# Gathering 80 instead of 72 expert rows early, eight instead of six per round, in a hybrid attention and retrieval layer

## The chip, the cores and the metric

The kernel runs on one core of a Trainium2 chip, in one launch. The metric is device time in microseconds, and lower is better. Engines are named as the profile names them: PE is TensorE (PEld its weight loads), DVE is VectorE, ACT is ScalarE, POOL is GpSimd and SP is SyncE.

## What is computed

One decoder layer on 512 tokens of width 1024, in float32:

```python
proj = x @ w_in                       # 1024 x 3072: q, k, v of two groups of 8 heads
oa = dilated_window_attention(qa, ka, va)   # windows (128,1), (512,4), (2048,16)
ob = stick_breaking_attention(qb, kb, vb)
x = layer_norm(ALPHA * x + concat(oa, ob) @ w_out)
# PEER: 8 heads, two top-16 of 128 keys each, then 16 of 256 sums
scores = einsum('bshpc,hpnc->bshpn', (x @ w_query), sub_keys)
expert_idx, gates = ...               # 8 x 16 = 128 of 16384 experts per token
h = einsum('td,ted->te', x, expert_u[expert_idx])
act = gates * gelu(h)
y = einsum('te,ted->td', act, expert_v[expert_idx])
x = layer_norm(ALPHA * x + y)
```

## The kernel before

The tokens are four blocks of 128. The experts are reached in two ways. For blocks 2 and 3 the whole tables `uT` and `peer_v` are streamed in 128 chunks of 128 experts each, and PE multiplies all of them (`h_mm` L969, `y_mm` L1318, with the gates spread out to a dense map). For blocks 0 and 1 only the chosen experts are fetched: each of a token block's 128 choices is one indirect gather of 128 rows (one row of 1024 floats per token, 512 KB in all), issued on POOL (L834), and DVE uses it in one instruction over 128x1024 elements: a dot product with x for `peer_u` (L852), a scaled addition for `peer_v` (L864). "A row" below is one such gather with its use. There are 512 of them, numbered in the order in which they are used: 0 to 127 are `peer_u` for block 0, 128 to 255 `peer_v` for block 0, and 256 to 511 the same for block 1. `issue()` keeps several gathers ahead of the use, as many as there are buffers less one: 7 buffers (pools `gat` and `g3`) for the early rows and 9 (`gat` and `g2`) later.

The rows are spread by hand over the other work of the kernel:

1. Input projection and attention of block 0, then its first routing. At its end the choices of block 0 are known and gathering can begin.
2. **The early stage**, which the change touches. The projection of blocks 1 to 3 (`project_in`, generator `proj`) loads the weights in pieces of 128x1024. For exactness in the fast PE format each piece is split in a high half on ACT (`wh`, L129) and a low half on DVE (`wl`, L133), and each product is three matmuls (L136, L137, L138, where L138 or L137 reads `wl`). Beside it the dilated heads of blocks 1 to 3 run (`heads_a`: PE L353, DVE L356, ACT L359, PE L363, ACT L366, PE L369), and the early rows are gathered and used. `mix` takes steps from the three in turn: `MIXB` gives how many of each, and `PRE0` how many rows are done in the stage. 18 rows are done before the mixing, the rest in it. `first_new` starts the first two stick-breaking heads.
3. The stick-breaking heads (PE L377 to L397, ACT L383 to L393, DVE L387), output projection (L575) and normalization, with 2 or 3 rows per step (`take`).
4. The query projection and the routing of blocks 1 to 3, with rows between the steps; chunks of `uT` are multiplied ahead.
5. **The final loop** over the chunks: per chunk `h_mm` of chunk c+36, `y_mm` of chunk c, the loads of a `uT` and a `peer_v` chunk, and as many rows as a proportion asks for (`goal`), so that all 512 are done by chunk 118. After chunk 91 there are no `uT` chunks left and only `y_mm` runs.

Between stages 2 and 5 the number of rows taken is fixed by the code: 160 of them. With 72 rows early, 232 are done when the final loop begins and 280 are left for it.

When row 127 has been used, the 128 dot products of block 0 go through Gelu in `close_dots` (ACT L842, with a table load before it and one after it, L844), and DVE multiplies them by the gates (L859) before it uses row 128. `close_dots` is called by the use of row 128, or in the code right after stage 3's heads, whichever is first.

Inside the early stage's mixing the order of each engine's instructions is set by the tile framework's own scheduler from the program's order; stages 3 to 5 are in the order written.

Of the kernel before, what the change touches and what calls it, by code (L numbers as in the profile page):

```python
# [79 lines left out]
TG = 4  # L80
LEAD = 36
KT = 6
MIXB = (6, 4, 4)
PRE0 = 72
QGATH = 3
QH = 2
PRE1 = 7
# [14 lines left out]
def build(ctx, nc, tc, a):  # L102
# [316 lines left out]
    def heads_a(tb, done):  # L419
        return heads(tb, done, head_a, close_a, 0)  # L420
# [72 lines left out]
    def until(main, side, ratio):  # L493
        n = 0
        for _ in main:
            n += 1
            while n >= ratio:
                n -= ratio
                next(side, None)

    def chain(*steps):
        for s_ in steps:
            yield from s_

    def run(*steps):
        ratio = steps[-1] if isinstance(steps[-1], tuple) else (1,) * len(steps)
        for _ in mix(*steps[:len(ratio)], ratio):
            pass

    def mix(*steps):  # L510
        ratio = steps[-1]
        live = [(s_, r) for s_, r in zip(steps, ratio)]
        while live:
            for s_, r in list(live):
                for _ in range(r):
                    if next(s_, s_) is s_:
                        live.remove((s_, r))
                        break
                    yield

    def head(steps, n):
        for _ in range(n):
            if next(steps, steps) is steps:
                return
            yield
# [299 lines left out]
    def gather(n):  # L825
        tb, kind, j = n // (2 * P), n // P % 2, n % P
        if n < PRE0:
            pool, nm, more = g3, "g3", GB3
# [42 lines left out]
    def issue():  # L871
        nonlocal issued
        ahead_ = GB1 + (GB2 if g2 else GB3 if issued < PRE0 else 0)
        while issued < min(done + ahead_ - 1, limit):
            gus[issued] = gather(issued)
            issued += 1

    def gathers(n):
        nonlocal done
        if n == PRE0:  # L880
            issue()
            yield
        while done < n:
            issue()
            gather_use(done, gus.pop(done))
            done += 1
            yield
# [165 lines left out]
    rest = []  # L1053
    limit = PRE0 + GB1 - 1
    early = gathers(PRE0)
    until(mix(route_steps(0, 4, 4), head(early, PRE1), (2, 1)), proj, 1)
# [15 lines left out]
    def first_new():  # L1072
        for j, n in ((0, 3), (1, 2)):
            begin(j)
            for _ in range(n):
                go(j)
            yield

    run(early, proj, chain(*(heads_a(tb, rest) for tb in PARTS[1]), first_new()), MIXB)
    qws.close()  # L1080
# [381 lines left out]
```

## Time and profile before

| | us |
|---|---|
| median of 3 runs | 1426.12 (1420.84 to 1427.63) |
| the profiled execution's own time | 1424.04 |
| its span | 1422.3 |
| PE busy in the span | 1366.6 (96%) |
| DVE busy | 1164.9 (82%) |
| POOL busy | 656.1 (46%) |
| moved by DMA | 497.16 MB, mean 350 GB/s |

The span is the profiled execution from its first to its last instruction; its own time includes 1.7 us around it. Busy shares are means over stages that have different limits, so the stages are read apart. Where the text quotes stretches of time, they count from the start of the span. In tables of stretches, the number after "x" counts the instructions in the stretch, "PEclk" is the granted TensorE clock as a share of full speed, and "DMA share" the mean busy share of the 16 DMA engines, which reaches 1.03 where they are full. In a timeline a bracket at a row's end tells how long the engine sat idle before the instruction and what ended that.

### The profile page before, as it was taken

How to read it: one execution, taken by the hardware profiler on the slowest of the kernel's cores; microseconds unless marked ns; L12 is line 12 of the kernel's file. 1: busy time of each engine (PE TensorE's matmuls, PEld its weight loads, DVE VectorE, ACT ScalarE, POOL GpSimd, SP SyncE). 2: the span in 40 equal slices, each digit the busy share in tenths (PEclk: the TensorE clock that was granted, in tenths of full speed). 3: DMA queues.
4: the chain of work that ended last, by engine and by line, in shares of the span. 5: the costliest groups of instructions: out<-in, count | busy, mean ns of one | idle time of the engine just before them, and what ended most of it. 6: DMA issues, size and time to landing. Idle time of an engine off the chain costs nothing.

```text
span 1422.3 us, 19497 instructions
## 1 busy us (share of the span) xinstructions
PE 1366.6 (96%) x6664; PEld 1100.6 (77%) x6664; DVE 1164.9 (82%) x2381; ACT 484.0 (34%) x1008; POOL 656.1 (46%) x526
## 2 busy tenths in 40 slices
PE   8999999999999999999999999999999999998897
PEld 4677877676679998888888888888778888886555
DVE  0269998869899999899988778778788878878888
ACT  1323344364411111899522222222222222214122
POOL 0003676668553332113465555555555555652520
PEclk9999999999999999999999999999999999999999
DMA  8798998799989998779999999999999999999792
GB/s 294 246 316 277 329 367 304 272 395 359 331 315 362 334 319 281 248 238 323 344 410 409 410 410 409 409 410 410 410 410 410 409 410 410 409 410 406 289 393 87
DMA packets 163874, 497.16 MB, mean 350 GB/s; under 512 B 16544, under 2 KB 48688, under 8 KB 163648
## 3 DMA queue, kind: packets, MB, share of 16 engines
q0 software_dynamic: 74304, 270.13, 50.1%
q1 hardware_dynamic: 87744, 220.16, 41.7%
q10 hardware_dynamic: 1728, 5.64, 1.0%
q8 instruction: 52, 0.85, 0.2%
q14 instruction: 46, 0.38, 0.1%
HBM read 478.83 MB, written 16.84 MB: 349 GB/s over the span
## 4 chain that ended last, share of the span: by engine, by line
DMA 36%; PE 35%; DVE 14%; issue 11%; POOL 2%; ACT 2%; SPq 0%; DVEq 0%; POOLq 0%; ACTq 0%
DMA g<-peer_u,eidx 17%; DMA g<-peer_v,eidx 16%; PE y L1318 6%; PE h L969 3%; PE a L685 3%; PE b L685 3%; PE m L280 2%; POOL g L834 2%; PE m L138 2%; PE m L137 2%; PE m L136 1%; DVE x L864 1%; DVE g L852 1%; DMA w<-peer_v 1%; DVE yg L864 1%
## 5 line engine op out<-in xcount | busy, mean ns | idle before, releaser
L834 POOL DMA_INDIRECT g<-peer_v,eidx x256 | 313.4, 1224 | 379.1 <-DVE yg L864 100.6
L834 POOL DMA_INDIRECT g<-peer_u,eidx x256 | 336.8, 1316 | 327.2 <-DVE topi L624 121.7
L969 PE MATMUL h<-xf,w 128*128 128x256 f32 x2048 | 470.5, 379 | 0.9 <-ACT gl L961 0.9
L969 PEld LDWEIGHTS h<-xf,w 128*128 128x128 f32 x2048 | 382.1, 190 | 52.6 <-ACT gl L961 1.3
L852 DVE SCALAR_TENSOR_TENSOR g<-g,x 128x1024 f32<-128x1024 f32 x256 | 307.5, 1221 | 75.0 <-DMA g<-peer_u,eidx 74.3
L1318 PE MATMUL y<-vh,a 128*128 128x512 f32 x864 | 270.2, 416 | 18.6 <-ACT a L1301 18.3
L1318 PEld LDWEIGHTS y<-vh,a 128*128 128x128 f32 x864 | 161.9, 190 | 62.8 <-ACT a L1301 25.0
L864 DVE SCALAR_TENSOR_TENSOR x<-g,hg,x 128x1024 f32<-128x1024 f32 x128 | 163.8, 1280 | 25.1 <-DMA g<-peer_v,eidx 24.1
L864 DVE SCALAR_TENSOR_TENSOR yg<-g,hg,yg 128x1024 f32<-128x1024 f32 x126 | 161.4, 1281 | 23.0 <-DMA g<-peer_v,eidx 22.8
L1301 ACT ACTIVATE a<-gl 128x512 fp32r<-128x512 f32 x54 | 34.0, 630 | 328.7 <-DVE gl L1291 328.7
L1318 PE MATMUL y<-vl,a 128*128 128x512 f32 x432 | 136.2, 397 | 0.0
L133 DVE TENSOR_TENSOR vl<-v,vh 128x1024 fp32r<-128x1024 f32 x105 | 128.0, 1219 | 9.1 <-ACT vh L1266 9.1
L1266 ACT ACTIVATE vh<-v 128x1024 fp32r<-128x1024 f32 x105 | 110.5, 1053 | 39.3 <-DMA v<-peer_v 32.0
L961 ACT ACTIVATE gl<-h 128x256 f32<-128x256 f32 x128 | 48.5, 379 | 151.5 <-PE h L969 151.3
L1318 PEld LDWEIGHTS y<-vl,a 128*128 128x128 f32 x432 | 80.8, 189 | 19.9 <-DVE vl L133 1.8
L935 ACT ACTIVATE o<-m,sg 128x128 f32<-128x128 f32 x256 | 75.1, 411 | 4.1 <-PE m L920 4.0
L926 DVE TENSOR_TENSOR o<-sg,c_small 128x512 f32<-128x512 f32 x64 | 43.9, 687 | 10.3 <-PE a L941 5.0
L280 PE MATMUL m<-w,x0f 128*128 128x256 f32 (+1 forms) x128 | 45.3, 504 | 6.3 <-DMA w<-w_in 6.3
L137 PE MATMUL m<-wl,x2h 128*128 128x512 f32 x96 | 39.0, 406 | 4.1 <-DVE wl L133 4.1
L1290 DVE TENSOR_TENSOR gl<-gl,gt 128x480 f32<-128x480 f32 x64 | 41.7, 652 | 0.0
L280 PEld LDWEIGHTS m<-w,x0f 128*128 128x128 f32 x128 | 23.8, 194 | 22.9 <-issue 15.4
L138 PE MATMUL m<-wh,x2l 128*128 128x512 f32 x96 | 38.5, 401 | 0.0
(312 smaller groups left out, 1859.5 us busy)
## 6 DMA issues: line engine op xcount, KB each, us to landing
w<-uT SPq DMA_DIRECT2D x128, 512.0 KB, 9.0
v<-peer_v SPq DMA_DIRECT2D x108, 512.0 KB, 7.5
w<-w_in SPq DMA_DIRECT2D x45, 512.0 KB, 5.2
gt<-gd SPq DMA_DIRECT2D x15, 960.0 KB, 13.0
w<-peer_wq SPq DMA_DIRECT2D x16, 512.0 KB, 5.3
wq<-peer_wq SPq DMA_DIRECT2D x16, 512.0 KB, 6.9
gd<-stage SPq DMA_DIRECT2D x15, 512.0 KB, 5.9
gd<-stage SPq DMA_DIRECT2D x15, 448.0 KB, 4.7
```

The lines of the kernel that those rows point to most:

```text
L133: nc.vector.tensor_sub(parts[1], src, parts[0].bitcast(F32))
L137: nc.tensor.matmul(ps, ah, bl, start=False, stop=False, **kw)
L138: nc.tensor.matmul(ps, al, bh, start=False, stop=last, **kw)
L280: nc.tensor.matmul(ps[:, ch * wd:(ch + 1) * wd], x0f[:, kk], w[:, k], start=kk == 0, stop=kk == KD - 1)
L685: nc.tensor.matmul(qps[it][:, sl], w, x_, start=fresh and kk == n == 0, stop=kk == KD - 1, skip_group_check=True)
L834: nc.gpsimd.indirect_dma_start(out=u, out_offset=None, in_=a["peer_v" if kind else "peer_u"], in_offset=bass.IndirectOffsetOnAxis(ap=eidx[ ...
L852: nc.vector.scalar_tensor_tensor(u, u, 1.0, x, op0=OP.mult, op1=OP.mult, accum_out=hs[:, j:j + 1])
L864: nc.vector.scalar_tensor_tensor(acc, u, hs[:, j:j + 1], acc, op0=OP.mult, op1=OP.add)
L935: nc.scalar.activation(hot[s][:, j], ps[:, j * P:(j + 1) * P], AF.Relu, scale=gate[tb][1][:, 1, t + j:t + j + 1])
L969: nc.tensor.matmul(hps[c][:, :ND], us[c][:, k], xf[:, k], start=k == 0, stop=k == KD - 1)
L1266: nc.scalar.activation(vsp[c][0], vs[c], AF.Copy)
L1318: nc.tensor.matmul(yps[t][hf], s_, w_[:, hf * 512:(hf + 1) * 512], start=c == 0 and n == 0, stop=c == P - 1 and n == len(terms) - 1)
```

## The change

Two numbers of the schedule are changed. 80 rows are done in the early stage instead of 72, and each turn of the mixing takes 8 of their steps instead of 6; the 4 projection steps and 4 head steps of a turn stay.

```diff
-MIXB = (6, 4, 4)
-PRE0 = 72
+MIXB = (8, 4, 4)
+PRE0 = 80
```

In the mixing there are then 62 rows instead of 54. Later takes stay as they are, so 240 rows are done when the final loop begins, and 272 are left for it.

**DVE, one turn of the early stage.** Before, from behind the first pair of heads to the low half of the next weight piece; `g` are gathered rows, `su` and `nm` the scores of a dilated head and their minimum, `x_100` the tokens.

```order
L852 SCALAR_TENSOR_TENSOR g,hg<-g,x_100 128x1024 x2
L356 ISA su,nm<-a,c_maska 128x256
L356 ISA nm 128x1
L356 ISA su,nm<-b,c_maska 128x256
L356 ISA nm 128x1
L852 SCALAR_TENSOR_TENSOR g_1564,hg<-g_1564,x_100 128x1024
L852 SCALAR_TENSOR_TENSOR g_1567,hg<-g_1567,x_100 128x1024
L852 SCALAR_TENSOR_TENSOR g,hg<-g,x_100 128x1024 x2
L133 TENSOR_TENSOR wl<-w,wh 128x1024
```

The same place on DVE after the change:

```order
L852 SCALAR_TENSOR_TENSOR g_1564,hg<-g_1564,x_100 128x1024
L852 SCALAR_TENSOR_TENSOR g_1567,hg<-g_1567,x_100 128x1024
L356 ISA su,nm<-a,c_maska 128x256
L356 ISA nm 128x1
L356 ISA su,nm<-b,c_maska 128x256
L356 ISA nm 128x1
L852 SCALAR_TENSOR_TENSOR g,hg<-g,x_100 128x1024 x5
L852 SCALAR_TENSOR_TENSOR g_1663,hg<-g_1663,x_100 128x1024
L133 TENSOR_TENSOR wl<-w,wh 128x1024
```

Two rows stand between the pairs of heads as before, and six instead of four between the second pair and the low half. The stretch ahead of this turn has eight rows instead of six before its low half. In the next turn one of the two rows more stands between the pairs and one behind them; in the two after that both stand behind the second pair.

**DVE, the end of the early stage.** Before, with the last two low halves (`wl`, x2); `o` is the output of the dilated heads, and `su` at L387 a stick-breaking head:

```order
L402 RECIPROCAL rz<-z 128x8
L852 SCALAR_TENSOR_TENSOR g,hg<-g,x_100 128x1024
L403 TENSOR_TENSOR o<-h,rz 128x512
L387 SCALAR_TENSOR_TENSOR su<-a,su 128x512
L852 SCALAR_TENSOR_TENSOR g_2168,hg<-g_2168,x_100 128x1024
L852 SCALAR_TENSOR_TENSOR g_2171,hg<-g_2171,x_100 128x1024
L852 SCALAR_TENSOR_TENSOR g,hg<-g,x_100 128x1024 x3
L133 TENSOR_TENSOR wl<-w,wh 128x1024 x2
L852 SCALAR_TENSOR_TENSOR g,hg<-g,x_100 128x1024 x2
L852 SCALAR_TENSOR_TENSOR g_2255,hg<-g_2255,x_100 128x1024
L852 SCALAR_TENSOR_TENSOR g_2258,hg<-g_2258,x_100 128x1024
L852 SCALAR_TENSOR_TENSOR g,hg<-g,x_100 128x1024 x2
```

After:

```order
L402 RECIPROCAL rz<-z 128x8
L387 SCALAR_TENSOR_TENSOR su<-a,su 128x512
L403 TENSOR_TENSOR o<-h,rz 128x512
L852 SCALAR_TENSOR_TENSOR g,hg<-g,x_100 128x1024
L852 SCALAR_TENSOR_TENSOR g_2210,hg<-g_2210,x_100 128x1024
L852 SCALAR_TENSOR_TENSOR g_2213,hg<-g_2213,x_100 128x1024
L852 SCALAR_TENSOR_TENSOR g,hg<-g,x_100 128x1024 x3
L133 TENSOR_TENSOR wl<-w,wh 128x1024 x2
L387 SCALAR_TENSOR_TENSOR su<-b,su 128x512
```

The six rows that stood behind the last two low halves are gone from there. In all, 14 rows more stand ahead of the last two low halves and 6 fewer behind them.

**ACT, stage 3.** Before, at the end of the stick-breaking heads (`su`), with the Gelu of block 0's dot products (`hg`) and the first lines of a normalization (`lw`):

```order
L393 ACTIVATE su<-b 128x256
L393 ACTIVATE su<-m_3004 128x256
L393 ACTIVATE su<-m_3028 128x256
L408 ACTIVATE o<-h 128x512
L432 ACTIVATE x_2379<-tr 128x512
L842 ACT_TABLE_LOAD
L842 ACTIVATE hg<-hg 128x128
L844 ACT_TABLE_LOAD
L175 ACTIVATE lw<-lw 128x1
L176 ACTIVATE lw<-lw 128x1
```

After:

```order
L393 ACTIVATE su<-a 128x256
L842 ACT_TABLE_LOAD
L842 ACTIVATE hg<-hg 128x128
L844 ACT_TABLE_LOAD
L383 ACTIVATE su<-m_3056 128x256
L384 ACTIVATE su<-su 128x256
L385 ACTIVATE su<-su,ones 128x256
L393 ACTIVATE su<-b 128x256
```

The Gelu with its two table loads now stands eight instructions earlier, ahead of the last head. On PE the order differs in the early stage alone, by the places of a few matmuls of the projection among those of the heads. SP issues the same transfers in the same order.

## Prediction

> **What bounds the kernel now.** I read the page first, then the chain of work that ended last, then tables of stretches for the two stages that the change touches, and last the timelines of PE and DVE around single waits.
>
> ```profile
> PE 1366.6 (96%) x6664; PEld 1100.6 (77%) x6664; DVE 1164.9 (82%) x2381; ACT 484.0 (34%) x1008; POOL 656.1 (46%) x526
> DMA  8798998799989998779999999999999999999792
> DMA 36%; PE 35%; DVE 14%; issue 11%; POOL 2%; ACT 2%; SPq 0%; DVEq 0%; POOLq 0%; ACTq 0%
> L852 DVE SCALAR_TENSOR_TENSOR g<-g,x 128x1024 f32<-128x1024 f32 x256 | 307.5, 1221 | 75.0 <-DMA g<-peer_u,eidx 74.3
> ```
>
> PE looks like the bound everywhere, but the chain gives as much to the DMA, and the slices show DMA full from about the middle on. The last row prices a `peer_u` row on DVE: 307.5/256 = 1.20 us.
>
> The final loop, by stretches, with its transfers and the first and last `h` matmul:
>
> ```profile
> 705.00:950.00 245.00, 243.61 (x1097) 206.84 (x1096) 197.37 (x283) 64.41 (x100) 138.43 (x106) 1.00 1.03 410
> 950.00:1290.00 340.00, 331.45 (x1477) 276.18 (x1476) 273.11 (x332) 85.27 (x136) 193.19 (x145) 1.00 1.03 410
> q0 software_dynamic: 36174, 131.72, 56.4%
> g<-peer_u,eidx POOLq DMA_INDIRECT x128, 17.2
> g<-peer_v,eidx POOLq DMA_INDIRECT x122, 17.8
> L969 PE MATMUL h<-xf,w x1469: 377/379/483, 704.8 to 1287.4; 128*128 128x256 f32 x184
> 712.16 3.45 PE h L969 x16
> 715.62 2.77 PE y L1318 x12
> ```
>
> Columns of the stretches: PE, PEld, DVE, ACT, POOL busy, then clock, DMA share, GB/s. DMA runs at 410 GB/s from end to end. PE misses 1.4 us up to 950 and 340 - 331.45 = 8.55 us after it: for a while the loop lives on chunks and rows loaded ahead, then it falls to the pace of DMA. The same from the other side: a chunk costs PE 3.45 + 2.77 = 6.22 us when nothing is late, so the 92 chunks with `h` need 572 us, and they took 583 (704.8 to 1287.4, and the last matmul): about 10.6 us lost. So this loop is bound by DMA by a hair, with PE close behind.
>
> The early stage, cut at the ends of the rows that stand ahead of each `wl` (I call the stretches turn 0 to turn 8):
>
> ```profile
> 177.00:187.20 10.20, 10.20 (x62) 9.31 (x61) 9.97 (x21) 4.00 (x7) 8.01 (x6) 1.00 1.02 408
> 187.20:198.00 10.80, 10.33 (x56) 7.87 (x55) 9.55 (x24) 4.91 (x14) 7.89 (x7) 1.00 1.00 381
> 198.00:209.00 11.00, 10.88 (x57) 7.98 (x56) 9.64 (x24) 5.46 (x15) 7.98 (x7) 1.00 0.95 346
> 209.00:221.40 12.40, 11.82 (x67) 9.32 (x65) 10.71 (x24) 7.14 (x16) 7.92 (x7) 1.00 0.91 331
> 221.40:233.40 12.00, 12.00 (x67) 9.20 (x66) 10.19 (x22) 5.96 (x14) 8.16 (x6) 1.00 0.90 305
> 233.40:247.00 13.60, 13.02 (x71) 9.61 (x70) 11.35 (x26) 5.96 (x12) 8.25 (x7) 1.00 0.88 299
> 247.00:261.50 14.50, 13.99 (x74) 9.28 (x74) 10.79 (x22) 5.82 (x15) 7.98 (x7) 1.00 0.71 238
> 261.50:273.70 12.20, 10.00 (x58) 8.09 (x57) 10.70 (x20) 6.46 (x10) 7.49 (x5) 1.00 0.79 264
> 273.70:283.00 9.30, 9.27 (x33) 7.26 (x33) 7.21 (x12) 1.13 (x2) 6.64 (x6) 0.82 0.87 303
> ```
>
> PE is nearly gapless here, DVE is full in turn 0 and has more air with each turn, as the heads grow longer on PE. Where DVE's rows meet PE:
>
> ```profile
> 188.44 0.62 PE L138 MATMUL m<-x2h,wl 128*128 128x384 f32 x2 [0.47 <-DVE wl L133]
> 191.84 0.42 DVE L356 CUSTOM_DVE_ANT_0 su<-a,c_maska 128x256 f32<-128x256 f32 x1 [0.47 <-PE a L353]
> 193.05 0.42 DVE L356 CUSTOM_DVE_ANT_0 su<-b,c_maska 128x256 f32<-128x256 f32 x1 [0.78 <-PE b L353]
> 208.91 1.22 DVE L133 TENSOR_TENSOR wl<-w,wh 128x1024 fp32r<-128x1024 f32 x1
> 211.10 0.52 PE L138 MATMUL m<-x2h,wl 128*128 128x384 f32 x2
> 221.36 1.22 DVE L133 TENSOR_TENSOR wl<-w,wh 128x1024 fp32r<-128x1024 f32 x1
> 223.43 0.52 PE L138 MATMUL m<-x2h,wl 128*128 128x384 f32 x2
> 233.42 1.22 DVE L133 TENSOR_TENSOR wl<-w,wh 128x1024 fp32r<-128x1024 f32 x1
> 236.46 0.51 PE L138 MATMUL m<-x2h,wl 128*128 128x384 f32 x2
> 272.46 2.35 DVE L133 TENSOR_TENSOR wl<-w,wh 128x1024 fp32r<-128x1024 f32 x2
> 273.73 0.50 PE L137 MATMUL m<-wl,x2h 128*128 128x512 f32 x1 [2.23 <-DVE wl L133]
> 275.05 0.63 PE L137 MATMUL m<-wl,x2h 128*128 128x512 f32 x1
> ```
>
> In turn 0 PE already waits 0.47 us for `wl`. Later the low half is done 1.0, 0.9 and 1.8 us before its first matmul (211.10 - 210.13, 223.43 - 222.58, 236.46 - 234.64). Behind the last rows PE waits 2.23 us.
>
> **The change, part by part.** *What it takes from the final loop.* A row there is 131.72/250 = 0.527 MB. Eight are 4.21 MB, or 10.3 us at 410 GB/s. The loop can't become faster than PE's own pace, which is 10.6 us away by the chunks and 8.55 us by the idle time after 950. With DMA full all the time, a chunk took 583/92 = 6.33 us; 10.3/92 = 0.11 less leaves 6.22, just PE's own pace, so that the lead that lasted to 950 lasts to about the end now. Of the two ends that meet there, 8.55 and 10.3, I take the middle, -9.5 us, since loads don't come evenly; the ends are -10.3 (all bytes) and -6 (PE waits for single late rows all the same, since DVE uses rows in order and `act_prep` stands behind them). DVE's 9.6 us saved there are worth nothing of their own: it is busy 197 of 245 us.
>
> *What it adds early.* Eight rows are 9.6 us of DVE, but it is their place that counts: 14 more stand ahead of the last `wl`, 6 fewer behind it, where the last projection matmuls cover them (turn 8), so that their leaving saves nothing. Turn by turn:
> - Turn 0, two rows more ahead of `wl`: DVE is busy 9.97 of 10.20 us and PE waits for it already. +2.4.
> - Turn 1: both stand behind the second pair of heads, while DVE's idle time (0.47 and 0.78 us) lies before that pair and waits for PE. Turn 0 and this one leave `wl` no slack. +2.4.
> - Turn 2: one row falls into the idle time before the pair; the other meets 1.0 us of slack. +0.3.
> - Turn 3: 2.4 against 0.9 of slack. +1.5. Turn 4: 2.4 against 1.8. +0.6.
> - Turns 5 and 6: DVE has 2.2 and 3.7 us of air, PE is the bound. 0.
> - Turn 7: as many rows as before, but all six stand behind L403, which waits for the last head, where one stood ahead of it. +1.2.
>
> Together 8.4. To this I add 1.0 for PE's clock: after the wait of 2.23 us the matmul at 275.05 took 0.63 us where the first one took 0.50, and turn 8 has a clock of 0.82, some 0.18 x 9.3 = 1.7 us lost; two new waits of that length may or may not bring as much (0 to 3.4). The Trainium skill ("TensorE: Matmul & The Clock Gate", "What's actually happening") has the clock halved after an idle window of about 3.4 us; no wait here is that long, so by that rule the 1.0 would be 0 and the sum lower by it. The trace shows a fall after 2.23 us, and I keep the 1.0.
>
> The early stage then costs +9.4. Its ends: +2.4 (turn 0 alone; the idle time of DVE in turns 1 to 7, 86.5 - 72.9 us by the rows above, takes the rest) and +16.8 (all 14 rows). A gain is excluded there, as nothing that PE waits for is removed.
>
> *What moves.* The Gelu and its table loads go from behind the heads to ahead of the last one.
>
> ```profile
> 387.66 7.03 PE L575 MATMUL m<-wo,x 128*128 128x512 f32 x16
> 388.48 1.28 ACT L842 ACT_TABLE_LOAD   x1
> 394.53 0.60 PE L186 MATMUL tr<-c_ident,x 128*128 128x128 f32 x4
> 375.61 0.39 ACT L383 ACTIVATE su<-m 128x256 f32<-128x256 f32 x1 [2.53 <-PE m L379]
> ```
>
> Before, 16 matmuls of 7.03 us covered them. In the new place ACT sat idle for 2.53 us waiting for PE, against 2.9 us of loads and Gelu (1.28 twice, and 0.31). Behind it on ACT stands the last head, and on DVE L859 and the rows; PE has two pieces of output projection to do meanwhile. 0, with ends of -1.3 and +1.3 (a table load either way). POOL issues the same gathers in the same order, eight of them from other buffers; SP's order is unchanged.
>
> The sum: -9.5 + 9.4 + 0 = -0.1 us on the profiled execution's 1424.04, so 1423.9. The median of the runs shown is 2.1 us above that execution, which gives 1426.0.
>
> **Rivals.** What can be told from no change here is about 0.5%, or 7 us.
>
> *Faster: the early air takes the rows.* If PE has enough matmuls that don't need `wl` to bridge turns 1 to 7 (the order on PE was moved for that), the early cost is turn 0's 2.4, and the loop's 9.5 stands: -7.1, 1419. For it speaks the 13.6 us of DVE air in turns 1 to 7, against it that it lies before the pairs, not where the rows were put.
>
> *Slower: gathers come too late.* POOL's issues in turns 1 to 7, and two single ones, the first beside DVE rows back to back, the second beside few:
>
> ```profile
> 187.20:273.70 86.50, 55.67 (x43) 1.00 0.87 306
> 270.21 1.99 POOL L834 DMA_INDIRECT g<-peer_u,eidx  x1 [0.30 <-issue]
> 290.10 0.94 POOL L834 DMA_INDIRECT g<-peer_u,eidx  x1 [0.30 <-issue]
> ```
>
> The mean is 1.29 us, with 0.30 between two: eight take 12.8 us, and a turn of mine lasts 13.2 (10.8 + 2.4). That just fits. With DVE fuller, more issues take 1.99. At a mean of 1.5 eight take 14.4: turns 1 to 5 grow by 3.6, 3.4, 2.0, 2.4 and 0.8, which with turns 0 and 7 and the clock is 16.8, and less the loop's 9.5 is +7.3: 1433. It decides from a mean of 1.34 on. Against it: of POOL's 31 idle us in this stretch 43 gaps of 0.30 are only 13, and 18 are left. The Trainium skill ("SBUF — State Buffer", "SBUF: two separate sides") says that a DVE instruction with two SBUF inputs and a GpSimd one exclude each other for a whole instruction, which is this rival's reason. The trace agrees in kind (0.94 against 1.99, about one row of DVE apart); by that rule alone, every issue waiting, eight would take 18 us.
>
> *The loop's gain is lost.* If PE waits for single late rows and not for bytes, the loop gives 3 us: +6.4, 1432. Against it: DMA is full in the whole loop.
>
> That the rows are not moved can be excluded from the code: 272 instead of 280 remain for the loop.
>
> **How the numbers follow.** Forecast 0.60 (within 0.5%); early air takes the rows 0.18 (faster by over 0.5%); late gathers 0.14 (slower by over 0.5%); gain lost 0.08, half of it over the mark. Faster 0.18, same 0.60 + 0.04 = 0.64, slower 0.14 + 0.04 = 0.18. The range reaches from just below the faster rival to just above the slower one, 1418 to 1435; the likeliest case alone, by the ends of single turns, the clock and the table loads, is 1421 to 1431.
>
> **What would show it.** Right: the first `h` matmul of the final loop later by 9 us (714 instead of 704.8), the last by nothing; turns 0 and 1 about 2.4 us longer with PE waiting for `wl` at L138; idle PE between 950 and 1290 nearly gone; and the heads' end in stage 3 unmoved against the early stage's end. Wrong: the loop beginning less than 5 us later (DVE's air was usable), or more than 13 later with DVE waiting for `peer_u` rows and POOL's mean above 1.34; or idle PE still above 5 us in the loop, which would say that bytes were not what it waited for.

## The result, and the profile after

The changed kernel takes 1438.65 us (median of 8 runs, 1430.02 to 1447.54) against 1425.66 of the kernel before in the same comparison: 1.0086 times as long, 95% interval 1.0067 to 1.0104. It is slower by 0.9%; the forecast was 1426.0, with a range to 1435. The profiled execution took 1440.02 us (span 1438.3).

The page of the changed kernel, with the lines that answer to those of before:

```profile
PE 1377.7 (96%) x6664; PEld 1110.8 (77%) x6664; DVE 1163.5 (81%) x2381; ACT 484.6 (34%) x1008; POOL 664.2 (46%) x526
DMA 36%; PE 29%; DVE 21%; issue 7%; ACT 4%; POOL 2%; another core or an unknown queue 0%; SPq 0%; DVEq 0%; ACTq 0%; POOLq 0%
L834 POOL DMA_INDIRECT g<-peer_u,eidx x256 | 345.1, 1348 | 328.7 <-DVE topi L624 123.2
```

The work is the same; DVE's share of the chain went from 14 to 21%, and the issue of a `peer_u` gather on POOL takes 1.35 us on the mean (before 1.32, from 336.8 us for the 256). The final loop by stretches, and where its `y` and `h` matmuls begin and end:

```profile
734.10:950.00 215.90, 215.90 (x973) 183.58 (x972) 173.45 (x256) 56.78 (x87) 124.61 (x91) 1.00 1.03 410
950.00:1302.00 352.00, 351.09 (x1578) 297.01 (x1577) 283.01 (x345) 90.50 (x142) 199.30 (x148) 1.00 1.03 410
L969 PE MATMUL h<-xf,w x2048: 377/379/634, 432.5 to 1302.0; 128*128 128x256 f32 x187
L1318 PE MATMUL y<-vh,a x864: 387/389/795, 734.1 to 1384.5; 128*128 128x512 f32 x173
```

PE's idle time after 950 fell from 8.55 us to 0.91 (352.00 - 351.09): the loop did what was forecast. But by its first `y` it began 25.0 us later (734.1; before 709.1), not 9, and its last `h` came at 1302.0 instead of 1287.4, where no change was forecast. The early stage, cut at the rows ahead of each `wl` as before, turn 0 to turn 8:

```profile
178.70:191.80 13.10, 11.39 (x66) 9.96 (x64) 12.21 (x22) 4.80 (x7) 10.46 (x8) 1.00 1.00 387
191.80:207.20 15.40, 14.11 (x52) 11.11 (x52) 11.83 (x26) 4.25 (x14) 9.86 (x8) 0.67 0.87 321
207.20:221.30 14.10, 12.23 (x61) 8.36 (x60) 12.12 (x28) 6.18 (x16) 11.36 (x10) 1.00 0.87 298
221.30:235.20 13.90, 12.31 (x66) 9.20 (x66) 12.91 (x28) 6.28 (x15) 9.93 (x8) 1.00 1.01 398
235.20:249.00 13.80, 12.52 (x65) 9.12 (x66) 12.54 (x26) 5.53 (x13) 11.62 (x8) 1.00 0.87 297
249.00:263.50 14.50, 13.19 (x70) 9.56 (x70) 13.65 (x28) 6.64 (x14) 11.82 (x9) 1.00 0.94 351
263.50:282.40 18.90, 18.15 (x84) 12.69 (x84) 13.07 (x28) 7.07 (x14) 11.18 (x9) 0.82 0.81 280
282.40:293.60 11.20, 6.83 (x38) 5.47 (x37) 10.35 (x19) 4.96 (x7) 7.02 (x6) 0.99 0.77 274
293.60:302.90 9.30, 9.02 (x33) 7.12 (x33) 4.25 (x7) 1.14 (x2) 3.66 (x3) 0.83 0.79 272
```

Turns 0 to 6 are all longer, and the granted clock (third number from the end) is 0.67 in turn 1 and 0.82 in turn 6, where it was 1.00. The timeline of PE shows the waits for `wl`, that of DVE the waits that the slowed heads cause in return:

```profile
193.09 0.62 PE L138 MATMUL m<-x2h,wl 128*128 128x384 f32 x2 [2.72 <-DVE wl L133]
222.53 0.62 PE L138 MATMUL m<-x2h,wl 128*128 128x384 f32 x2 [1.84 <-DVE wl L133]
293.88 0.80 PE L137 MATMUL m<-wl,x2h 128*128 128x512 f32 x1 [4.65 <-DVE wl L133]
```

```profile
197.82 0.42 DVE L356 CUSTOM_DVE_ANT_0 su<-a,c_maska 128x256 f32<-128x256 f32 x1 [1.81 <-PE a L353]
200.01 0.42 DVE L356 CUSTOM_DVE_ANT_0 su<-b,c_maska 128x256 f32<-128x256 f32 x1 [1.76 <-PE b L353]
267.82 0.69 DVE L356 CUSTOM_DVE_ANT_0 su<-b,c_maska 128x512 f32<-128x512 f32 x1 [2.47 <-PE b L353]
275.07 0.69 DVE L356 CUSTOM_DVE_ANT_0 su<-a,c_maska 128x512 f32<-128x512 f32 x1 [3.12 <-PE a L353]
```

So each engine waits for the other in turn. The whole stretch from `wl` to the last `wl`, before and then after, says how much of DVE's air was used:

```profile
178.60:272.50 93.90, 90.63 (x487) 69.21 (x486) 80.09 (x162) 44.19 (x96) 61.05 (x47) 1.00 0.89 317
```

```profile
180.20:292.60 112.40, 99.23 (x487) 74.00 (x485) 96.18 (x188) 44.39 (x96) 80.79 (x60) 0.92 0.89 325
```

DVE has 16.1 us more to do, and its idle time is 16.2 us instead of 13.8: in sum none of the air was used up.

To compare kernels I put their profiled executions side by side, with the first gather as zero (it falls between 125.8 and 128.7, ahead of every change of the schedule). Times in us; "last `wl`" is where DVE begins the last two low halves, which stand back to back, 1.1 us apart; only in dense_only and no_use they stand apart, and there it is the begin of the very last one (before 147.3, changed 165.9). "end" is the span less the first gather; the last column is the comparison over all runs, each kernel with runs of the kernel before from its own session.

| kernel | last `wl` | first query matmul | first `y` | `y` to end | end | median | ratio to before, 95% |
|---|---|---|---|---|---|---|---|
| before | 146.2 | 276.5 | 582.8 | 713.2 | 1296.0 | 1425.66 | 1 |
| changed | 164.8 | 297.8 | 606.3 | 704.2 | 1310.5 | 1438.65 | 1.0086 (1.0067 to 1.0104) |
| loop_less8 | 145.8 | 276.4 | 581.9 | 702.9 | 1284.8 | 1417.18 | 0.9929 (0.9903 to 0.9955) |
| rows_only | 145.8 | 288.0 | 592.2 | 702.8 | 1295.0 | 1426.56 | 1.0007 (0.9989 to 1.0025) |
| dense_only | 164.8 | 293.5 | 599.5 | 714.8 | 1314.3 | 1439.25 | 1.0080 (1.0050 to 1.0109) |
| warm | 166.8 | 296.3 | 600.6 | 702.0 | 1302.6 | 1432.03 | 1.0046 (1.0023 to 1.0068) |
| no_use | 151.9 | 284.7 | 589.4 | 703.4 | 1292.8 | 1422.02 | 0.9970 (0.9957 to 0.9983) |
| turn0_only | 150.2 | 278.9 | 585.0 | 715.4 | 1300.4 | 1431.34 | 1.0049 (1.0031 to 1.0067) |
| turn0_warm | 151.0 | 279.7 | 585.9 | 712.0 | 1297.9 | 1427.65 | 1.0011 (0.9997 to 1.0026) |
| split44 | 182.5 | 312.8 | 617.0 | 703.3 | 1320.3 | 1447.06 | 1.0142 (1.0120 to 1.0165) |
| stage3 | 147.9 | 293.2 | 599.1 | 703.7 | 1302.8 | 1424.42 | 0.9997 (0.9981 to 1.0012) |
| late8 | 150.9 | 284.2 | 588.5 | 706.0 | 1294.5 | 1423.18 | 0.9977 (0.9963 to 0.9992) |
| stage5 | 146.4 | 276.6 | 592.1 | 699.4 | 1291.5 | 1422.07 | 0.9967 (0.9952 to 0.9983) |
| both4 | 148.6 | 280.1 | 585.8 | 704.0 | 1289.8 | 1421.84 | 0.9977 (0.9964 to 0.9990) |

The changed kernel's 16.0 us of span over the kernel before are: 1.5 ahead of the first gather, 21.3 in the early stage and stage 3 (18.6 of them before the last `wl`), 2.2 between the first query matmul and the first `y`, and -9.0 in the loop.

### The profile page after: what moved, and what is told of

Read it like the earlier page. It is cut to its first block, busy times and chain, and to the rows that moved or that the text cites. A ratio compares the mean times of both kernels' runs of the same rounds, so it can differ in the third digit from the quotient of the medians.

```text
span 1438.3 us, 19493 instructions
## 1 busy us (share of the span) xinstructions
PE 1377.7 (96%) x6664; PEld 1110.8 (77%) x6664; DVE 1163.5 (81%) x2381; ACT 484.6 (34%) x1008; POOL 664.2 (46%) x526
## 4 chain that ended last, share of the span: by engine, by line
DMA 36%; PE 29%; DVE 21%; issue 7%; ACT 4%; POOL 2%; another core or an unknown queue 0%; SPq 0%; DVEq 0%; ACTq 0%; POOLq 0%
DMA g<-peer_u,eidx 18%; DMA g<-peer_v,eidx 14%; PE y L1318 6%; PE h L969 5%; DVE yg L864 3%; DVE x L864 3%; PE m L280 3%; POOL g L834 2%; DVE g L852 2%; PE m L575 1%; ACT o L935 1%; DMA v<-peer_v 1%; DVE topi L624 1%; DVE s L620 1%; DMA w<-peer_v 1%
## 5 line engine op out<-in xcount | busy, mean ns | idle before, releaser
L834 POOL DMA_INDIRECT g<-peer_u,eidx x256 | 345.1, 1348 | 328.7 <-DVE topi L624 123.2
L1318 PEld LDWEIGHTS y<-vh,a 128*128 128x128 f32 x864 | 163.8, 191 | 50.1 <-ACT a L1301 13.8
L138 PE MATMUL m<-wh,x2l 128*128 128x512 f32 x96 | 39.1, 407 | 0.0
```

Of the source, the lines that this page charges most:

```text
L834: nc.gpsimd.indirect_dma_start(out=u, out_offset=None, in_=a["peer_v" if kind else "peer_u"], in_offset=bass.IndirectOffsetOnAxis(ap=eidx[ ...
L1318: nc.tensor.matmul(yps[t][hf], s_, w_[:, hf * 512:(hf + 1) * 512], start=c == 0 and n == 0, stop=c == P - 1 and n == len(terms) - 1)
```

## The experiments

Theory 1 was that each wait of PE for `wl` lowers its clock, and that the slow heads then hold up DVE. Rival A was that a row simply costs its 1.2 us wherever it stands in the early stage; rival B, that load lowers the clock and not waits; rival C, late gathers; rival D, that later turns take up with DVE's idle time what one turn loses. "DVE's air" is that idle time.

### The loop's term by itself: loop_less8

```diff
-NG = 4 * P
+NG = 4 * P - 8
-        if kind and j == P - 1:
+        if kind and (j == P - 1 or n == NG - 1):
```

> The kernel before with the last eight peer_v rows neither gathered nor used, so that the final loop has 272 rows left as in the changed kernel and nothing is added early (the sums of the second block lack those rows). If the loop's term is right (-9.5, ends -6 and -10.3): 1414 to 1420, first h matmul of the loop unmoved, last h matmul 9 to 10.5 us earlier. If the loop had gained only because it began late: 1422 to 1426.

1417.18, ratio 0.9929; `y` to end 702.9 instead of 713.2, and the loop begins where it did. Eight rows are worth 10 us there, by themselves. The changed kernel got them too, so by the medians all the rest of the change costs some 23 us (13.0 + 10), where 9.4 was forecast.

### Eight a round without the extra rows, and the extra rows without eight a round: dense_only, rows_only

```diff
# dense_only
-MIXB = (6, 4, 4)
+MIXB = (8, 4, 4)
# rows_only
-PRE0 = 72
+PRE0 = 80
```

> 8 a round, but 72 rows: the rows are all used by turn 6, and the loop keeps its 280. PE's order is nearly that of the changed kernel. Theory 1: turns 0 to 6 as long as in the changed kernel (together +15 to +19 us), with PEclk 0.5 to 0.9 in 190 to 205 and in 265 to 275; turns 7 and 8 without rows have no wait for the last wl and give back 3 to 5; time 1435 to 1440. Rival A (only the number of rows ahead of the last wl counts, six more: +7.2): 1432 to 1434, whatever the clock.

> 80 rows, but 6 a round as before: the eight more come behind the last turn. PE's order is that of the kernel before. Theory 1: turns 0 to 7 as before the change (the last wl around 273), no new drop of PEclk before 275; the eight rows stand on DVE ahead of stage 3's first heads and cost there between 3 and 9.6 us; the loop gives back 10. Time 1419 to 1427. Rival A (a row costs its 1.2 us wherever it stands in the early stage): +9.6 - 10.4, 1425. Rival C (80 rows in flight are too many for POOL and the buffers): the stage ends as late as in the changed kernel, 1435 to 1440.

Density is the loss: with 72 rows, eight a round, the very last `wl` comes nearly as late as in the changed kernel (164.8; changed 165.9, before 147.3), and the time is 1439.25. Turns 0 to 6, with 54 rows instead of 42, lasted 102.9 us instead of 82.9, as long as the same turns with 56 rows in the changed kernel (102.2). From there to the very last `wl`, a stretch in which no early rows were left, it took 9.6 us instead of 12.1: of the 20.0 us only 2.5 came back (theory 1: 15 to 19, and 3 to 5 back), and PE had no idle time there. Rival A, which counted six more rows ahead of the last `wl` at 1.2 us each, was 10 us short. In rows_only the turns stayed as they were, and the eight rows stood ahead of the first heads of stage 3. PE's timeline there:

```profile
297.93 2.07 PE L389 MATMUL b<-su,c_tri 128*128 128x512 f32 x2 [7.99 <-DVE su L387]
```

One wait of 7.99 us, and a clock of 0.50 to 0.63 behind it (295 to 305): 11.5 us at the first query matmul, about what the loop gave back. The result lies within what theory 1 expected and near rival A's figure, so it does not tell them apart; rival C's 1435 to 1440 it excludes.

### The clock: warm, turn0_only, turn0_warm

Matmuls by a zero matrix fill the time in which PE waited, at chosen chunks of the input projection (15 is the one at the end of turn 0):

```diff
+WARM = {15: 12, 16: 8, 17: 8, 18: 5, 20: 4, 22: 18}
...
+        for _ in range(warm[0]):
+            nc.tensor.matmul(ps, zero, bh, start=False, stop=False, **kw)
         nc.tensor.matmul(ps, ah, bl, start=False, stop=False, **kw)
+        for _ in range(warm[1]):
+            nc.tensor.matmul(ps, zero, bh, start=False, stop=False, **kw)
```

Of the pair `warm`, one is the number from `WARM` where a chunk first needs `wl`, the other is 0.

> The changed kernel, with matmuls by a zero matrix added (they add nothing to the result) where PE waited for a low half: 12, 8, 8 and 5 ahead of the first wl matmuls of turns 1 to 4, 4 near the end of turn 5, 18 ahead of the last wl. They fill the waits and load no other engine. Theory 1 (each wait lowers the clock that PE is granted for some 8 us, and the slow heads then hold up DVE): PEclk stays at 0.95 or more from 180 to 300, the early stage ends 6 to 9 us earlier than in the changed kernel (about 295 instead of 302.9), time 1429 to 1433. Rival A (the extra rows cost what they take on DVE, 14 x 1.2 = 16.8, and the clock merely follows the waits): PEclk rises too, but the stage ends within 2 us of 302.9, time 1436 to 1440. Rival B (the clock is lowered by load, not by waits): PEclk falls as before, time 1438 to 1443.

The time fell to 1432.03, but not as theory 1 had it. The first wait was 0.68 instead of 2.72 us and turn 1 ran at a clock of 1.00, yet it still lasted 14.4 us (15.4 in the changed kernel, 10.8 before). Its own wait grew to 2.59 us at 205.20, where I had put too few matmuls, and the clock fell behind that one. The last `wl` was no earlier (166.8). What was won is behind it: PE waited 0.47 instead of 4.65 us, at a clock of 1.00 up to 305. But this run can't divide the cost between clock and rows. The added matmuls are work for PE too, and turns 2 to 4 lasted 15.5, 16.1 and 15.0 us where the changed kernel took 14.0, 14.0 and 13.8; in turn 1 DVE waited 1.19 us for a gathered row. And of the 7.9 us by which this execution is shorter than that of the changed kernel, only 1.5 lie ahead of the first query matmul; the rest lies in stages that the edit doesn't touch. Rival B isn't excluded either: the clock fell again to 0.50 between 237.5 and 240 and to 0.58 after 267.5, behind waits of 1.33 and 0.75 us. To price the clock apart from the rows, one dense round alone, on the kernel before, and the same with 12 matmuls in its one wait (`chain(...)` is shortened):

```diff
# turn0_only; turn0_warm has WARM = {15: 12} and the added matmuls as well
-    run(early, proj, chain(...), MIXB)
+    news = chain(...)
+    run(head(early, 8), head(proj, 4), head(news, 4), (8, 4, 4))
+    run(early, proj, news, MIXB)
```

> The kernel before (72 rows, 6 a round), with 8 rows in the first round alone; PE's order is that of before but for two matmuls. One long wait for wl at the end of turn 0, and nothing else. Theory 1: the wait of 2.5 to 3 us brings PEclk to 0.5 to 0.7 for 8 to 10 us, so that turn 0 is 3 us longer and turn 1 another 2 to 3 us, though it has no row more; 1430 to 1433. Rival A (two rows, 2.4, and the clock's fall costs nothing): turn 0 2.4 to 3 longer, turn 1 within 0.5 of 10.8; 1428 to 1430. Rival D (later turns take it up with their air on DVE): the last wl within 1 us of before, 1425 to 1427.5.

> The kernel with one dense round (turn0_only), with 12 matmuls by a zero matrix in the place where PE waited 2.42 us for wl; nothing else moves on PE or DVE. If that wait itself lowers the clock and the slow heads behind it cost 1.3 us in turn 1 (12.13 instead of 10.81 there): PEclk 1.00 from 190 to 200, turn 1 10.7 to 11.0, the last wl 1.3 us earlier against the first gather (150.2 instead of 147.1 of before becomes about 149), time 1428 to 1431. If turn 1's growth has another cause (rows shifted on DVE): PEclk 1.00 and turn 1 still 11.8 to 12.4, 1430 to 1433.

The first three turns by stretches, and PE's wait, of turn0_only:

```profile
180.20:191.60 11.40, 9.94 (x56) 8.56 (x54) 10.80 (x20) 3.47 (x5) 8.77 (x8) 1.00 1.01 395
191.60:203.70 12.10, 10.85 (x51) 8.75 (x52) 9.53 (x22) 3.89 (x13) 7.87 (x7) 0.86 0.98 355
203.70:214.60 10.90, 10.69 (x54) 7.48 (x53) 9.55 (x22) 5.48 (x15) 7.88 (x7) 1.00 0.93 332
```

```profile
192.85 0.61 PE L138 MATMUL m<-x2h,wl 128*128 128x384 f32 x2 [2.42 <-DVE wl L133]
```

And the same stretches of turn0_warm:

```profile
180.30:192.10 11.80, 11.79 (x68) 10.71 (x66) 10.76 (x18) 3.48 (x5) 9.17 (x8) 1.00 0.98 378
192.10:202.95 10.85, 9.55 (x51) 7.41 (x52) 9.59 (x24) 3.90 (x13) 7.93 (x7) 1.00 0.97 362
202.95:213.90 10.95, 10.74 (x54) 7.55 (x53) 9.58 (x24) 5.48 (x15) 7.92 (x7) 1.00 0.99 357
```

```profile
193.40 0.61 PE L143 MATMUL m<-x2h,wl 128*128 128x384 f32 x2 [1.31 <-DVE wl L134]
```

This is the clean pair, with one profiled execution of each. Two rows make turn 0 2.9 us longer (11.4 from `wl` to `wl`; before 8.5). The wait of 2.42 us brings the clock to 0.86 in turn 1, which has no row more and still lasts 12.1 instead of 10.8. With the wait cut to 1.31 us the clock is 1.00 and turn 1 lasts 10.85, as before. So this wait cost 1.3 us more, after its end. Rival D is out: in turn0_only the last `wl` is 4.0 us late, and no later turn made any of that up. The last `wl` of turn0_warm, expected 1.3 us earlier, came 0.8 later: turn 0 took 0.4 more (with six rows it varied from 8.2 to 8.8 over these kernels), and turn 4 lasted 13.6 instead of 12.1, with a clock of 0.50 from 227.5 to 230 and no wait of PE over 0.31 us in the 11 us ahead of it. The added matmuls needn't be the cause: stage3, whose early stage is that of the kernel before, has the same turn 4 (13.6 us, a clock of 0.50 from 225 to 227.5). The medians (1431.34 and 1427.65) lie further apart than 1.3. In these two executions the end of the loop, where only `y` runs, differs by 3.9 us: from the last `h` to the last `y` turn0_only took 129.4 us at a clock of 0.93, turn0_warm 125.5 at 0.97. Nothing in the edits reaches that far, and why the clock differs there is open.

### Whether DVE's air can take a row: late8, split44, stage3

```diff
# late8, on the changed kernel (chain(...) is shortened here and in split44)
-    run(early, proj, chain(...), MIXB)
+    news = chain(...)
+    run(head(early, 30), head(proj, 20), head(news, 20), (6, 4, 4))
+    run(early, proj, news, MIXB)
# split44, on the changed kernel
-MIXB = (8, 4, 4)
+MIXB = (4, 4, 4, 4)
-    run(early, proj, chain(...), MIXB)
+    run(early, proj, early, chain(...), MIXB)
# stage3, on the kernel before
-            take(3 if 10 <= i < 18 else 2 if i <= NTASK else 0)
+            take(3 if 2 <= i < 18 else 2 if i <= NTASK else 0)
```

> 80 rows, 6 in each of the first five rounds and 8 in each of the last, where DVE had the most idle time before (2.2 to 3.7 us a turn). The prediction had these turns take two more rows for nothing: last wl as before the change, loop -10, 1416 to 1419. If a row costs its 1.2 us there too, since only 3 of DVE's 17 gaps in these turns (0.14 to 1.90 us) are as long as a row: six rows ahead of the last wl, turns 5 to 7 each 2 to 4 us longer, 1424 to 1430, with the clock's fall in 1427 to 1432.

Turns 5 to 7 of late8 by stretches, and the wait at their end:

```profile
234.00:249.90 15.90, 15.32 (x83) 11.08 (x81) 13.64 (x30) 6.65 (x14) 10.23 (x8) 1.00 0.82 272
249.90:265.50 15.60, 15.01 (x82) 10.52 (x82) 12.97 (x28) 7.08 (x14) 10.00 (x9) 1.00 0.88 303
265.50:278.10 12.60, 6.86 (x38) 5.51 (x37) 11.75 (x21) 4.97 (x7) 9.35 (x7) 0.97 0.87 294
```

```profile
279.39 0.80 PE L137 MATMUL m<-wl,x2h 128*128 128x512 f32 x1 [7.04 <-DVE wl L133]
```

At a clock of 1.00, 1.00 and 0.97, turns 5, 6 and 7 lasted 2.3, 1.1 and 1.7 us more for two rows each (before 13.55, 14.55 and 10.94). Six rows ahead of the last `wl` made it 4.8 us late, 0.8 each: cheaper than in the first turns, not free. DVE's idle time in these turns fell only from 7.5 to 5.7 us, though six rows are about 7 us of work. As the loop gave back more (7.2 in this execution, whose end with `y` alone ran at 0.93 like that of turn0_only), the kernel became faster, 0.9977. DVE's timeline before the change suggests why the air doesn't take more. Its 13.6 us of idle time in turns 1 to 7 are 17 gaps, and these three are the only ones as long as a row (the next is 1.19):

```profile
241.86 0.69 DVE L356 CUSTOM_DVE_ANT_0 su<-a,c_maska 128x512 f32<-128x512 f32 x1 [1.90 <-PE a L353]
252.45 0.69 DVE L356 CUSTOM_DVE_ANT_0 su<-b,c_maska 128x512 f32<-128x512 f32 x1 [1.65 <-PE b L353]
265.21 0.69 DVE L403 TENSOR_TENSOR o<-h,rz 128x512 f32<-128x512 f32 x1 [1.27 <-PE h L369]
```

All end in a wait for PE's heads, and a row put into a smaller gap would make the head behind it late. This reading fits late8 and the changed kernel; no run changed the gaps themselves.

> The changed kernel with its eight rows of a round in two halves, four ahead of the projection's steps and four ahead of the heads'. The same rows in the same turns, but on DVE one or two fewer ahead of wl in most turns. If it is the place of wl that costs (theory 1: wait, then clock): waits of PE for wl under 1 us, PEclk near 1.0, turns 0 to 7 together 98 to 104 us, 1424 to 1430. If DVE and PE wait for each other by turns, so that a row costs its 1.2 us wherever it stands in a turn (rival A): 110 to 114 us, 1434 to 1440.

Neither came true. `wl` was moved ahead of one or two rows in most turns, so those rows now stood ahead of the heads' L356, and PE waited for the heads (197.78, 2.38 us; 228.97, 1.30) instead of for `wl`. Its stretch to the last but two `wl`:

```profile
179.70:298.30 118.60, 106.86 (x431) 78.24 (x429) 81.96 (x166) 36.67 (x85) 74.16 (x54) 0.77 0.79 274
```

A mean clock of 0.77, DVE idle for 36.6 us, and the worst time of all, 1447.06. PE's order was not quite that of the changed kernel, so this isn't the place alone; but a kernel in which PE hardly waited for `wl` in these turns was the slowest of all. Whether the low clock or the place of the rows made it so slow, this run can't say.

> The kernel before (72 rows, 6 a round) with eight rows more used in stage 3, one more in each of steps 2 to 9; nothing added early, 272 left for the loop. DVE was busy 5.7 to 8.1 of each 10 us there, without PE waiting for it. If that air can be used: heads' end later by 0 to 2 us, 1416 to 1420. If a row costs its 1.2 us there as well: 1424 to 1428.

A row costs its time in stage 3 as well: the median is that of before (0.9997), though the loop gained 9.5 in the profiled execution. PE's timeline has waits for DVE that were not there:

```profile
306.71 2.08 PE L389 MATMUL a<-su,c_tri 128*128 128x512 f32 x2 [2.66 <-DVE su L387]
327.40 0.91 PE L389 MATMUL a<-su,c_tri 128*128 128x384 f32 x2 [1.66 <-DVE su L387]
372.06 1.11 PE L186 MATMUL tr<-c_ident,x 128*128 128x128 f32 x4 [3.49 <-DVE x L597]
```

That execution was the longest of its 12 (1432.42), so its sums in the table are above the typical ones.

### Late gathers: no_use

```diff
+SKIP = [r + 8 * t for t in range(7) for r in (24, 25)]
...
+    nc.vector.memset(hg, 0.0)
...
+        if n in SKIP:
+            return
         if kind == 0:
             nc.vector.scalar_tensor_tensor(u, u, 1.0, x, ...)
```

> The changed kernel, in which the two last peer_u rows of each of the first seven rounds (14 rows) are gathered but not used: their scalar_tensor_tensor is left out, and their dot products are zero. POOL, the queue and the buffers carry what they do in the changed kernel, DVE what it did before; the order on PE differs a little from both. Theory 1 and rival A (the cost comes from DVE's rows): turns 0 to 7 last 94 to 97 us together as before the change (93.8; changed kernel 112.5), and since the loop's 10 stay, the time is 1415 to 1421. Rival C (gathers come too late): turns as in the changed kernel, time 1434 to 1440.

The stretch of the turns:

```profile
179.70:279.20 99.50, 96.62 (x497) 74.06 (x496) 72.40 (x145) 43.59 (x96) 62.59 (x53) 0.95 0.91 330
```

99.5 us to the very last `wl`, with a clock of 0.95, where the changed kernel took 113.6 and the kernel before 95.0: most of the loss goes when DVE's rows go, and the gathers alone don't bring it. POOL's mean issue was 62.59/53 = 1.18 us, against 80.79/60 = 1.35 in the changed kernel: the slow issues follow from DVE's rows. The rest, 4.6 us over the kernel before, and the time of 1422.02 above what was expected, are not clean: the order differs, with 58 rows ahead of the very last `wl` instead of the 66 of the kernel before, a new wait of PE of 2.64 us for the heads in turn 1 and one of 6.06 us behind rows at the start of stage 3. In turn 1 DVE also waited 4.2 us for gathered rows, so a part of this rest can be rival C's.

### A better place: stage5, both4

```diff
# stage5, on the kernel before; both4 has s % 6 == 5, PRE0 = 76,
# and 8 rows instead of 6 in the sixth and seventh round
             g_mm(s)
+            if s < 24 and s % 3 == 2:
+                take(1)
```

> The kernel before with eight peer_v rows more used between 575 and 615 us, one in every third step of the loop that spreads the gates, where ACT is busy 9.7 to 9.9 of 10 us, DVE 8.5 to 9.6 and POOL not at all; 272 left for the final loop. If ACT is the bound there and DVE's row fits beside it: that stretch longer by 0 to 3 us, loop -10, 1416 to 1420. If DVE, PE and ACT wait for each other by turns and a row costs 1.2 us here as well: 1424 to 1427.

Two stretches of that loop, before and then in stage5:

```profile
580.00:600.00 20.00, 18.91 (x132) 16.74 (x131) 17.16 (x78) 19.60 (x59) 0.00 (x0) 1.00 0.68 230
600.00:620.00 20.00, 18.88 (x126) 16.10 (x125) 18.62 (x39) 18.51 (x62) 0.00 (x0) 1.00 0.47 140
```

```profile
580.00:600.00 20.00, 19.09 (x131) 16.67 (x130) 19.51 (x84) 18.66 (x54) 3.62 (x3) 1.00 0.95 308
600.00:620.00 20.00, 16.24 (x107) 13.57 (x107) 19.39 (x35) 17.63 (x59) 3.77 (x3) 1.00 0.73 221
```

DVE fills up and PE and ACT lose some of it. The kernel is 4.6 us faster than before (0.9967). But the rows are no cheaper here: in the profiled execution the first `y` is 9.3 us later, eight rows at 1.2 each, with the first query matmul unmoved. What makes this place the better one by that execution is the loop, which gave back 13.8 us (699.4 instead of 713.2) and not the 10.3 of loop_less8. Why it gave more is open.

> The two places that were cheapest, with half the rows in each: 76 rows early, with 8 instead of 6 in the sixth and seventh round alone, and four peer_v rows more in the loop that spreads the gates, one in every sixth step; 272 left for the final loop, whose 10 us are gained as in the others. Eight rows cost 6.5 us in the late rounds alone (loop 10, time -3.5) and 5.4 in the gates' loop alone (-4.6). If the cost goes with the number of rows: half of each, 5.9, time 1421 to 1423.5. If fewer rows in a place fit into more of its gaps: 2 to 4, time 1418 to 1421. If rows left to the end of the early stage wait there as with late8: 1423 to 1426.

1421.84, 0.9977: half the rows in each of two places cost about as much as all of them in one, so no gain by spreading can be seen; PE waited 4.67 us for the last `wl` (before 2.23). stage5, late8 and both4 are all a little faster than the kernel before by intervals that exclude 1; among them the order isn't settled.

## Why the prediction was wrong

The step that failed is the one that booked DVE's idle time as room. For turns 2, 5 and 6 it put six rows at 0.3 us together; they cost 8.4, some 3 of it the clock's. The second is the term for the clock, put at 1.0 where about 4 is the nearest the runs give. No case with a chance of its own stood for all 14 rows at full price: that was only an end (-9.5 + 16.8 = +7.3, 1433). Point by point, lengths from `wl` to `wl`:

- *The loop, -9.5*: right. -9.0 in the changed kernel, -10.3 in loop_less8, and idle PE after 950 nearly gone (0.91 us), as the middle of 8.55 and 10.3 said. From the first `y` to the last `h` the changed kernel saved 10.4 and lost 1.4 behind it.
- *Turns 0 and 1, +2.4 each*: the mechanism right, PE waiting for `wl` at L138. Turn 0 +3.1, turn 1 +4.6, part of that the clock.
- *Turn 2, where a row "falls into the idle time before the pair", and turns 5 and 6, where "DVE has 2.2 and 3.7 us of air"*: this step failed. +3.1, +1.0 and +4.3 instead of +0.3, 0 and 0; late8 has +2.3 and +1.1 for turns 5 and 6 at full clock. A sum of idle time was taken for room. Before the change it lay in 17 pieces of 0.14 to 1.90 us that, all but one, ended in a wait for PE, and the prediction had quoted two of them (0.47 and 0.78) without asking whether 1.2 fits.
- *Turn 3, +1.5; turn 4, +0.6; turn 7, +1.2*: +1.5, +1.8 and -0.7. Together with the others, +18.6 to the last `wl` where 8.4 was put.
- *The clock, +1.0, ends 0 to 3.4*: the second term that was mis-sized. The clock was lowered in turns 1 and 6 alone, which are 8.9 us longer together, so it can hardly have cost more than that; turns 0, 2 to 5 and 7, at a clock of 0.99 or 1.00, are 9.7 longer. Turn 6 lasted 18.8 us in the changed kernel and 15.6 with the same eight rows at full clock (late8): 3.2. Turn 1 lasted 15.4, and 14.4 at full clock (warm): 1.0, with matmuls added in that one. That makes about 4 of the 18.6; the other 14 are 14 rows at about 1 us. This division rests on turns of different executions, each profiled once, and isn't shown; that the fall behind one wait cost 1.3 is what the clean pair shows. And the larger fall, in turn 6, stood behind no wait for `wl`: the longest waits of PE ahead of it were 0.94 and 0.75 us, for ACT.
- *Six rows fewer behind the last `wl`*: they saved nothing, as said, but PE's wait there grew from 2.23 to 4.65 us, and that wait was not in the sum.
- *The upper end of the early stage, +16.8*: "all 14 rows" was the right row to take, nearer than the 9.4 chosen between the ends. The stage cost 21.3, beyond that end, which left out the clock and PE's longer wait for the last `wl`.
- *The Gelu and its table loads, 0*: right within what can be read. From the last `wl` to the first query matmul 133.0 us instead of 130.3, of which 2.4 are the longer wait for `wl`.
- *Late gathers*: the marks that the prediction set for it were half met (the loop more than 13 us later, POOL's mean 1.35), and it was still not the cause. DVE waited for gathered rows for 2.2 us between 176 and 304 (before 9.3), and in no_use the issues became faster when DVE's rows were left out.
- *Between the first query matmul and the loop*: +2.2 that nobody forecast. rows_only has the same rows done there and took 2.1 less than before, so it is scatter as far as these runs tell.

## What to carry to other kernels

Before idle time is booked as room, list its gaps: an instruction longer than the gap can make the partner late, so that the wait comes back a turn later. Where two engines hand work to each other in short turns, take an added instruction at close to its full length, unless a single gap covers it (here 0.5 to 1.6 us a row, by turns at full clock, and 1.0 on the mean), and give the clock behind new waits of PE a range of its own. Test the gain and the cost of a move apart (rows left out at one end, rows added at the other): the gain here was real, about 10 us, and every place that was tried for the rows took at least half of it back.

## What the runs showed of the hardware

PE's granted clock falls behind waits that are shorter than I had thought, and for a time that varies. In turn0_only a wait of 2.42 us was followed by 0.69 and 0.63 in the stretches of 2.5 us from 192.5 on, and then 1.00; in the changed kernel a wait of 2.72 us in the same place by 0.50 from 195 to 202.5. In split44, whose longest wait in the turns before 298 was 2.38 us, the mean was 0.77. Nor does every such wait bring a fall: PE waited 2.23 to 2.26 us for the last `wl` in seven of these executions, and the clock fell to 0.50 or 0.54 behind it in four (before, loop_less8, rows_only, stage5), while it stayed at 1.00 in the other three (turn0_only, turn0_warm, stage3). The Trainium skill ("TensorE: Matmul & The Clock Gate", "What's actually happening") has the clock halved after an idle window of about 3.4 us that runs freely. The halving agrees (0.50 in these stretches), the length doesn't: none of these waits was that long, and in turn0_warm the clock fell to 0.50 at 227.5 with no wait over 0.31 us in the 11 us ahead of it. stage3 has such a fall at 225 with no added matmuls. What else lowers it is open.
